# A backbone layer on one core: where the scans' loads lie, when the inverse's rounds are issued, and one lasting slot for wide weights

## The chip, the cores and the metric

One Trainium2 chip, one of its cores. The metric is the device time of one execution in microseconds. The kernel before ran three times: 1548.43, 1549.96 and 1550.71 us, median 1549.96 us.

## The reference, cut to what matters

One layer over 1024 latent tokens and 256 context tokens of width 1024. All products are in float32 precision (the kernel splits each float32 operand into a high and a low part and multiplies three times).

```python
px = modulate(rms_norm(x, norm1_w), sh1, sc1) @ w_in      # latent, 3600 columns
pc = modulate(rms_norm(ctx, norm1_w), csh1, csc1) @ w_in  # context
# group A: gated DeltaNet, 4 heads of 128
q, k, v = SiLU(conv5(...)); q, k = l2_normalize(q), l2_normalize(k); z, a, b from the same projection
m = where(strict_lower, (b*k) @ k.T * decay, 0)           # per chunk
u, w = solve(I + m, ...)                                  # triangular, per chunk and direction
S, o = scan over chunks, forward and backward, context first
dn_x = rms_norm(o_f + o_b) * silu(z)
# group B: 8 heads of 64, a query sees an 8 x 16 window of the 64-wide grid and all context keys
na_x = softmax([q k_win + rpb, q k_ctx]) @ [v_win, v_ctx]
x = x + g1 * (concat(dn_x, na_x) @ w_out)
x = x + g2 * swiglu(modulate(rms_norm(x, norm2_w), sh2, sc2), w_ffn_in, w_ffn_out)
```

## The kernel before, in words

**Stages.** The kernel projects all tokens in a list of jobs, then runs the two scans with the window attention filled in between, then multiplies with `w_out`, and then runs the feed-forward part.

**Jobs.** `jobs` is a list. A `Block` is one block of 128 output columns for all tokens (conv blocks `k`, `q`, `v`, and attention blocks `nk`, `nq`); a `Wide` is 256 columns with tokens on the partitions (`z`, half 1 then half 0, and the attention's values `nv`, halves 0 and 1). The order is: k0, k1, k2, k3, z1, nk0, nk1, nk2, nv0, nk3, q0 to q3, nq0 to nq3, v0, nv1, v1, v2, v3, z0. At job n the weights of job n+1 are fetched (`prefetch`: a load on SP's queue into `wraw`, which has one buffer, then a high part by ACT and a low part by POOL), the matmuls of job n run, job n-1 is normed (`norm`) and the Block two back is finished (`finish`).

**Norm and finish.** `norm` of an `nk` block makes three matmuls of sums (line 492), each into a PSUM bank called `m`, of which there are two, and ACT takes the logarithm of each (line 493). `finish` of a `v` block transposes it (line 527), scales it on DVE (line 531) and stores it to `v_d` (line 535). `kx`, `cr`, `cacc` and `zt` are the convolution's buffers, in a pool `cp`.

**Background.** Between the matmuls of a job one step of a background generator is issued (two or three per tile of a `Wide`). First comes `block_inverses`: decay tables, 32x32 blocks, then 30 rounds of substitution on DVE in the tile `N` (lines 885 and 887; two rounds a step), transposes of `N` by TensorE (line 897), and stores to `x_d`. Then comes `preps`: for each of 10 chunks it builds masked decays (`rg` on POOL, line 957; a matmul into a bank `pr`, lines 967 and 968) and assembles inverse blocks (lines 987 and 998), stored to `at_d` and `y_d` (line 1010). The chunks after the first two wait until the four `q` blocks are in the set `done`.

**Wide weights.** z1, nv0 and nv1 take their split weights `zw` from a pool `zp`, which is closed together with the background's other pools (`late`) when v3 begins. Then a pool `sp1` is opened, in which z0's `zw` is placed (and after it, in the same slot, the scans' sum `oacc`), then the attention's first loads are issued (`next(fill)`), then z0's weights are fetched.

**Values for the attention.** After nv1, 64 DMAs on SP copy `nv_d` to `vw_d` in windows (line 1108), all four pairs of heads each.

**Scans.** The pools of the scans are placed over the freed projection pools: `sl` (loads) first, then `sw` (working tiles, and the loads of `v`). The first chunk of each direction begins with a product of `v` and `y` (line 1217); the loads are line 1165.

**Order.** The framework plans the order of each engine's and each queue's instructions from the order in the program and from when it takes each to be ready; on the chip each engine and each queue then keeps that order and waits in place.

Of the kernel before, what the change touches and what calls it, by code (L numbers as in the profile page):

```python
# [88 lines left out]
def hybrid(ctx, tc, a, dbg):  # L89
# [47 lines left out]
    mr = const("mr", [128, 5, 128], F32R)  # L137
    mneg = const("mneg", [128, 2, 128], F32R)

# [235 lines left out]
    with ExitStack() as bs:  # L375
# [32 lines left out]
        class Block:  # L408
# [64 lines left out]
            def norm(self):  # L473
# [8 lines left out]
                if kind == "q":  # L482
# [6 lines left out]
                    return  # L489
                for s0, n in self.segs:  # L490
                    p = bank()
                    pe.matmul(p[:, :n], M[C_BD2], r[:, s0:s0 + n], start=True, stop=True)
                    act.activation(r[:, s0:s0 + n], p[:, :n], AF.Ln, bias=b_eps, scale=1.0 / ND)
# [26 lines left out]
            def finish(self):  # L520
                kind, acc, i = self.kind, self.acc, self.i
                if kind in "kv":
                    vt = cp.tile([128, NCH, 128], F32, name="vt", tag="kx", bufs=3)
                    for g, m in ((0, 4), (4, 4), (8, 2)):
                        p = bank()
                        for c in range(m):
                            pe.transpose(p[:, c * 128:(c + 1) * 128], acc[:, (g + c) * 128:(g + c + 1) * 128], ident)
                        if kind == "k":
                            act.copy(vt[:, g:g + m].rearrange("p c d -> p (c d)"), p[:, :m * 128])
                        else:  # L530
                            dve.tensor_tensor(vt[:, g:g + m], p[:, :m * 128].rearrange("p (c d) -> p c d", d=128),
                                              SV[:, g:g + m, i:i + 1].to_broadcast([128, m, 128]), OP.mult)
                        yield
                    dst = v_d if kind == "v" else k_d
                    sp.dma_start(dst[:, i * 128:(i + 1) * 128].rearrange("(c p) d -> p c d", p=128), vt)
                if kind == "q":
# [27 lines left out]
        class Wide:  # L564


            def __init__(self, kind, half, zp):
                self.kind, self.half, self.zp = kind, half, zp
                self.n = 272 if kind == "z" and half else 256
                self.lasting = kind == "z" and not half  # L570

            def room(self):
                w = self.zp().tile([128, 2, KT, 256 if self.lasting else 272], F32R, name="zw", tag="zw")
                self.hi, self.lo = w[:, 0], w[:, 1]

            def prefetch(self):
                h2, n = 2 * self.half, self.n // 2
                src = a["w_nv"] if self.kind == "nv" else a["w_z%d" % self.half]
                if self.kind == "z":
                    h2 = 0  # L580
                if not self.lasting:
                    self.room()
                for i in range(2):
                    raw = wp.tile([128, KT, 136], F32, name="wraw", tag="wraw", bufs=1)
                    r, s = raw[:, :, :n], slice(i * n, i * n + n)
                    sp.dma_start(r, src[h2 + i])
                    act.copy(self.hi[:, :, s], r)
                    pool.tensor_tensor(self.lo[:, :, s], r, self.hi[:, :, s].bitcast(F32), OP.subtract)
# [10 lines left out]
            def tiles(self):  # L599
# [18 lines left out]
                for t in range(2, NCH):  # L618
                    p = self.wide(t, 0, self.n)
                    if half == 0:  # L620
                        if t % 4 == 2:
                            zg = cp.tile([128, NCH, 128], F32, name="zg", tag="kx", bufs=3)
                            zg = zg.rearrange("p a b -> p (a b)")[:, :1024]
                        act.copy(zg[:, (t - 2) % 4 * 256:(t - 2) % 4 * 256 + 256], p[:, :256])
# [19 lines left out]
        with ExitStack() as xs:  # L644
# [65 lines left out]
            with tc.manual_schedule(engines={mybir.EngineType.PE, mybir.EngineType.DVE, mybir.EngineType.Activation}):  # L710
# [30 lines left out]
                for k in range(1, KT):  # L741
# [12 lines left out]
                    if k == 5:  # L754
                        act.copy(mr[:, 4], ident)
                        for d in range(2):
                            act.mul(mneg[:, d], masks[:, d], -1.0e30)
                        act.copy(mr[:, 0:4], masks)

        cp = pools(bs, "cp", "right")  # L760
        late = ExitStack()
        adp = pools(late, "adp", "left")
        zpool = [pools(late, "zp", "left")]
        first_half = ExitStack()
        cpa = pools(first_half, "cpa", "left")
        WK = cpa.tile([128, 2, NU, 32], F32, name="WK", tag="WK")
        KKc = WK[:, 1]

        def zp():
            return zpool[0]  # L770

# [53 lines left out]
        def block_inverses():  # L825
            with ExitStack() as gs:
# [55 lines left out]
                for c in range(30, 0, -1):  # L882
# [4 lines left out]
                    dve.tensor_tensor(N[:P, :, 0:c, c + 1:32], N[:P, :, 0:c, c + 1:32], t, OP.add)  # L887
                    if c % 2:
                        yield
                flat = N.rearrange("p b r c -> p b (r c)")  # L890
                dve.memset(flat[:P, :, 0:1024:33], 1.0)
                yield
                U = WK.rearrange("p d u i -> p (d u) i")
# [23 lines left out]
        def preps():  # L917

            first_half.close()
            with ExitStack() as gs:  # L920
# [28 lines left out]
                def prep(i, got):  # L949
# [9 lines left out]
                    for d, c, kk, xc, at in got:  # L959
                        for q in q32:  # L960
                            act.copy(fxs[d][q, :, q], xc[q, 1])
                    yield 1
                    es = []
                    for d, c, kk, xc, at in got:
# [64 lines left out]

        jobs = first + [Block("k", 2), Block("k", 3), Wide("z", 1, zp)]  # L1030
        inv = len(jobs)
        jobs += [Block("nk", i) for i in range(3)] + [Wide("nv", 0, zp), Block("nk", 3)]
        turn = len(jobs)
        jobs += [Block("q", i) for i in range(4)]
        later = len(jobs)
        queries = range(turn, later)
        jobs += [Block("nq", i) for i in range(4)] + [Block("v", 0), Wide("nv", 1, zp)]
        values = len(jobs) - 1
        jobs += [Block("v", i) for i in (1, 2, 3)] + [Wide("z", 0, zp)]

# [11 lines left out]
        for n in range(2, len(jobs) + 2):  # L1052
# [7 lines left out]
            if n == len(jobs) - 2:  # L1060
                bg.drain()
                bg2.drain()
                late.close()
                sp1 = pools(middle, "sp1", "left")
                zpool[0] = sp1
                jobs[n + 1].room()
                fill = attention(pools(attn, "nw", "left", 2))
                next(fill)
# [22 lines left out]
            elif j:  # L1091
                for k in range(KT):
                    j.mm([k])
                    if k >= 3:
                        next(fin, 0)
                    bg.step(1)
# [5 lines left out]
            done.add(n - 2)  # L1102
            if isinstance(j, Wide) and n == values:
                vlat = nv_d[CT:].rearrange("(r c) d -> r c d", c=64)
                for cb in range(4):
                    for ch in range(4):
                        for r in range(4):
                            sp.dma_start(vw_d[r * 32:r * 32 + 32, :, cb, ch],
                                         vlat[4 * ch + r, BLKS[cb]:BLKS[cb] + 32].rearrange("c (h d) -> c h d", d=128))
            if nrm:  # L1110
# [30 lines left out]

    with ExitStack() as gs:
        sl = pools(gs, "sl", "right", 3)
        shift(gs, "spad", "right", 16)
        sw = pools(gs, "sw", "right", 2)
        gs.callback(scan_psum.close)
# [14 lines left out]
        def load(d, c, near):  # L1161

            def tile_of(name, src):
                t = work(name, 3) if name == "v" else sl.tile([128, 4, 128], F32, name=name, tag=name)
                sp.dma_start(fl(t), src)
# [612 lines left out]
```

## Time and profile before

| | |
|---|---|
| median of three runs | 1549.96 us |
| the profiled execution | 1549.54 us |
| its span, first to last instruction | 1547.5 us |
| TensorE (PE) busy | 1479.8 us, 96% |
| VectorE (DVE) busy | 994.3 us, 64% |
| ScalarE (ACT) busy | 727.7 us, 47% |
| GpSimd (POOL) busy | 233.6 us, 15% |
| mean granted clock of TensorE | 0.982 |

A view by windows gives for each stretch of the span how long each engine was busy, the granted clock of TensorE (PEclk, 1.00 is full) and the share of the DMA engines in use. In a timeline, each row is: start, duration, engine, line, operation, tiles written <- tiles read, shapes, and in brackets how long the engine had been idle before and what ended that. SPq and ACTq are the queues from which SP and ACT issue DMAs.

### The profile page before, as it was taken

How to read it: one execution, taken by the hardware profiler on the slowest of the kernel's cores; microseconds unless marked ns; L12 is line 12 of the kernel's file. 1: busy time of each engine (PE TensorE's matmuls, PEld its weight loads, DVE VectorE, ACT ScalarE, POOL GpSimd, SP SyncE). 2: the span in 40 equal slices, each digit the busy share in tenths (PEclk: the TensorE clock that was granted, in tenths of full speed). 3: DMA queues.
4: the chain of work that ended last, by engine and by line, in shares of the span. 5: the costliest groups of instructions: out<-in, count | busy, mean ns of one | idle time of the engine just before them, and what ended most of it. 6: DMA issues, size and time to landing. Idle time of an engine off the chain costs nothing. (4 is left out here: it accounts for less than half of the span.)

```text
span 1547.5 us, 23963 instructions
## 1 busy us (share of the span) xinstructions
PE 1479.8 (96%) x8702; PEld 1235.2 (80%) x8702; DVE 994.3 (64%) x1712; ACT 727.7 (47%) x1404; POOL 233.6 (15%) x286
## 2 busy tenths in 40 slices
PE   6999999899989978999999999999999999999998
PEld 3788787678778867888887878888888888888887
DVE  5774497675554543777986469866665556599652
ACT  5442552635764235666773166333333334354440
POOL 1154500733554010111210000000000000000000
PEclk9999999999999979999999999999999999999999
DMA  9274221577556467899637502632323324698742
GB/s 389 64 217 133 67 72 63 163 212 241 182 169 212 130 174 237 283 288 261 220 102 255 208 34 82 211 102 103 103 102 103 109 100 159 231 381 279 244 144 82
DMA packets 204118, 267.35 MB, mean 173 GB/s; under 512 B 16736, under 2 KB 114528, under 8 KB 202976
## 3 DMA queue, kind: packets, MB, share of 16 engines
q1 hardware_dynamic: 198480, 261.07, 51.7%
q10 hardware_dynamic: 5520, 4.76, 0.9%
q8 instruction: 68, 1.11, 0.3%
q14 instruction: 50, 0.41, 0.1%
HBM read 201.02 MB, written 68.94 MB: 174 GB/s over the span
## 5 line engine op out<-in xcount | busy, mean ns | idle before, releaser
L405 PE MATMUL blk<-hh,whi 128*128 128x512 f32 (+1 forms) x410 | 123.4, 395 | 2.3 <-ACT kk L550 1.4
L1415 ACT CAST uhi<-wq 128x512 fp32r<-128x512 f32 x101 | 61.0, 622 | 133.5 <-issue 84.6
L1415 ACT CAST uhi<-ws 128x512 fp32r<-128x512 f32 x91 | 53.9, 621 | 147.3 <-PE ps L1354 92.9
L405 PE MATMUL blk<-hl,whi 128*128 128x512 f32 (+1 forms) x410 | 116.8, 377 | 0.3 <-DVE hl L707 0.3
L595 PE MATMUL blk<-zw,hh 128*128 128x256 f32 (+1 forms) x576 | 115.0, 293 | 1.3 <-ACT kk L550 1.1
L405 PE MATMUL blk<-hh,wlo 128*128 128x512 f32 (+1 forms) x410 | 114.7, 377 | 0.6 <-POOL wlo L200 0.6
L1416 DVE TENSOR_TENSOR ulo<-wq,uhi 128x512 fp32r<-128x512 f32 x101 | 67.4, 687 | 59.1 <-ACT uhi L1415 34.0
L1354 PE MATMUL ps<-hT,uhi 128*128 128x512 f32 x336 | 103.7, 390 | 0.0
L1354 PE MATMUL ps<-hT,ulo 128*128 128x512 f32 x336 | 103.5, 389 | 0.0
L1354 PE MATMUL ps<-lT,uhi 128*128 128x512 f32 x336 | 103.4, 389 | 0.0
L595 PEld LDWEIGHTS blk<-zw,hh 128*128 128x128 f32 x576 | 92.8, 192 | 5.2 <-ACT kk L550 1.4
L1354 PE MATMUL ps<-hB,uhi 128*128 128x512 f32 x288 | 89.2, 391 | 0.6 <-ACT hB L1529 0.6
L1354 PE MATMUL ps<-lB,uhi 128*128 128x512 f32 x288 | 88.7, 389 | 0.4 <-DVE lB L1530 0.4
L1354 PE MATMUL ps<-hB,ulo 128*128 128x512 f32 x288 | 88.7, 389 | 0.0
L405 PEld LDWEIGHTS blk<-hh,wlo 128*128 128x128 f32 x410 | 72.6, 192 | 15.3 <-POOL wlo L200 0.9
L405 PEld LDWEIGHTS blk<-hl,whi 128*128 128x128 f32 x410 | 72.4, 191 | 14.5 <-DVE hl L707 0.8
L405 PEld LDWEIGHTS blk<-hh,whi 128*128 128x128 f32 x410 | 69.4, 194 | 18.2 <-issue 4.5
L595 PE MATMUL blk<-zw,hl 128*128 128x256 f32 (+1 forms) x288 | 83.2, 289 | 0.0
L1354 PEld LDWEIGHTS ps<-lT,uhi 128*128 128x128 f32 x336 | 63.1, 188 | 13.1
L1354 PEld LDWEIGHTS ps<-hT,ulo 128*128 128x128 f32 x336 | 63.1, 188 | 13.1
L1354 PEld LDWEIGHTS ps<-hT,uhi 128*128 128x128 f32 x336 | 62.9, 188 | 13.0
L200 POOL TENSOR_TENSOR wlo<-wraw,whi 128x1024 fp32r<-128x1024 f32 x18 | 44.7, 2485 | 179.2 <-ACT whi L199 160.7
(359 smaller groups left out, 3540.5 us busy)
## 6 DMA issues: line engine op xcount, KB each, us to landing
wq<-w_fo SPq DMA_DIRECT2D x99, 256.0 KB, 4.2
wq<-w_gu SPq DMA_DIRECT2D x88, 256.0 KB, 2.9
wad<-wa SPq DMA_DIRECT2D x64, 256.0 KB, 4.4
bt<-rpb SPq DMA_DIRECT2D x64, 192.0 KB, 3.8
t_d<-g SPq DMA_DIRECT2D x22, 512.0 KB, 3.6
fr<-t_d SPq DMA_DIRECT2D x44, 256.0 KB, 5.0
f_d<-g SPq DMA_DIRECT2D x33, 256.0 KB, 2.1
fr<-f_d SPq DMA_DIRECT2D x33, 256.0 KB, 3.8
```

The source lines that it names most:

```text
L200: lo_engine.tensor_tensor(o, r, h.bitcast(F32), OP.subtract)
L405: pe.matmul(o, ww[:, k], xx[k][:, s], start=k == 0 and j == 0, stop=k == KT - 1 and j == 2)
L595: pe.matmul(p[:, :c1 - c0], x[k][:, s], ww[:, k, c0:c1], start=k == 0 and j == 0, stop=k == KT - 1 and j == 2)
L1354: pe.matmul(o, w[wi][:, k], x[xi][:, k], start=first and k == 0 and j == 0, stop=k == n - 1 and j == 2, skip_group_check=True)
L1415: act.copy(hi, self.raw[key])
L1416: dve.tensor_tensor(lo, self.raw[key], hi.bitcast(F32), OP.subtract)
```

## The change

It makes these edits:

- The third segment of an `nk` norm uses a bank `pr` instead of a third turn of the two `m` banks.
- `v` blocks are stored to `v_d` from ACT's queue; `k` blocks stay on SP's.
- All four `Wide` jobs take `zw` from one pool `sp1`, opened before the background's pools and lasting to the end of the scans, in one slot of 272 columns. The tile `mneg` moves from the constants to the pool of the modulation.
- z0's output tile `zg` moves from the buffers `kx` to the buffers `cr`.
- The inverse issues one round a step instead of two, and has four empty steps instead of one before the transposes of `N`.
- The first prep has one more empty step before its first matmul.
- A block counts as done when its `finish` is exhausted, instead of at the end of the job.
- The copies to `vw_d` are made in two halves: 64 DMAs after nv0 for two pairs of heads, 64 after nv1 for the other two.
- In the scans, `sw` is placed first and `sl` after it, so that `sl` lies over `cp`; `v` moves from `sw` to `sl`, three buffers as before.

```diff
-                for s0, n in self.segs:
-                    p = bank()
+                for j, (s0, n) in enumerate(self.segs):
+                    p = bank("pr" if j == 2 else "m")
                     pe.matmul(p[:, :n], M[C_BD2], r[:, s0:s0 + n], start=True, stop=True)
...
-                    sp.dma_start(dst[:, i * 128:(i + 1) * 128].rearrange("(c p) d -> p c d", p=128), vt)
+                    (act if kind == "v" else sp).dma_start(dst[:, i * 128:(i + 1) * 128].rearrange("(c p) d -> p c d", p=128), vt)
...
             def room(self):
-                w = self.zp().tile([128, 2, KT, 256 if self.lasting else 272], F32R, name="zw", tag="zw")
+                w = sp1.tile([128, 2, KT, 272], F32R, name="zw", tag="zw")
...
-                if not self.lasting:
-                    self.room()
+                self.room()
...
-                            zg = cp.tile([128, NCH, 128], F32, name="zg", tag="kx", bufs=3)
-                            zg = zg.rearrange("p a b -> p (a b)")[:, :1024]
+                            zg = cp.tile([128, T], F32, name="zg", tag="cr", bufs=2)
+                            zg = zg[:, :1024]
...
         late = ExitStack()
+        sp1 = pools(middle, "sp1", "left")
         adp = pools(late, "adp", "left")
-        zpool = [pools(late, "zp", "left")]
+        mneg = adp.tile([128, 2, 128], F32R, name="mneg", tag="mneg")
+        for d in range(2):
+            act.mul(mneg[:, d], mr[:, d].bitcast(F32), -1.0e30)
...
                     dve.tensor_tensor(N[:P, :, 0:c, c + 1:32], N[:P, :, 0:c, c + 1:32], t, OP.add)
-                    if c % 2:
-                        yield
+                    yield
                 flat = N.rearrange("p b r c -> p b (r c)")
                 dve.memset(flat[:P, :, 0:1024:33], 1.0)
-                yield
+                for _ in range(4):
+                    yield
...
                     yield 1
+                    if i == 0:
+                        yield 1
                     es = []
...
                 late.close()
-                sp1 = pools(middle, "sp1", "left")
-                zpool[0] = sp1
-                jobs[n + 1].room()
                 fill = attention(pools(attn, "nw", "left", 2))
...
-                    if k >= 3:
-                        next(fin, 0)
+                    if k >= 3 and next(fin, 0) == 0:
+                        done.add(n - 2)
...
-            if isinstance(j, Wide) and n == values:
+            if isinstance(j, Wide) and j.kind == "nv":
+                hv = slice(2 * j.half, 2 * j.half + 2)
                 vlat = nv_d[CT:].rearrange("(r c) d -> r c d", c=64)
                 for cb in range(4):
                     for ch in range(4):
                         for r in range(4):
-                            sp.dma_start(vw_d[r * 32:r * 32 + 32, :, cb, ch],
-                                         vlat[4 * ch + r, BLKS[cb]:BLKS[cb] + 32].rearrange("c (h d) -> c h d", d=128))
+                            rows = vlat[4 * ch + r, BLKS[cb]:BLKS[cb] + 32].rearrange("c (h d) -> c h d", d=128)
+                            sp.dma_start(vw_d[r * 32:r * 32 + 32, hv, cb, ch], rows[:, hv])
...
     with ExitStack() as gs:
+        sw = pools(gs, "sw", "right", 2)
+        shift(gs, "spad", "right", 16)
         sl = pools(gs, "sl", "right", 3)
-        shift(gs, "spad", "right", 16)
-        sw = pools(gs, "sw", "right", 2)
...
-                t = work(name, 3) if name == "v" else sl.tile([128, 4, 128], F32, name=name, tag=name)
+                t = sl.tile([128, 4, 128], F32, name=name, tag=name)
```

More of the change, by code (lines that the diff above doesn't have):

```diff
@@ L137, in hybrid @@
     mr = const("mr", [128, 5, 128], F32R)
-    mneg = const("mneg", [128, 2, 128], F32R)
     v_d = dram.tile([T, 512], F32, name="v_d", tag="v_d")
@@ L564, in hybrid, with __init__ @@
         class Wide:
-            def __init__(self, kind, half, zp):
-                self.kind, self.half, self.zp = kind, half, zp
+            def __init__(self, kind, half):
+                self.kind, self.half = kind, half
                 self.n = 272 if kind == "z" and half else 256
-                self.lasting = kind == "z" and not half
             def room(self):
-                w = self.zp().tile([128, 2, KT, 256 if self.lasting else 272], F32R, name="zw", tag="zw")
+                w = sp1.tile([128, 2, KT, 272], F32R, name="zw", tag="zw")
                 self.hi, self.lo = w[:, 0], w[:, 1]
@@ L755, in hybrid @@
                         act.copy(mr[:, 4], ident)
-                        for d in range(2):
-                            act.mul(mneg[:, d], masks[:, d], -1.0e30)
                         act.copy(mr[:, 0:4], masks)
@@ L767, in hybrid @@
         KKc = WK[:, 1]
-        def zp():
-            return zpool[0]
         def decay_tables(gp):
@@ L1028, in preps @@
                 flush(tick[0] + 2)
-        jobs = first + [Block("k", 2), Block("k", 3), Wide("z", 1, zp)]
+        jobs = first + [Block("k", 2), Block("k", 3), Wide("z", 1)]
         inv = len(jobs)
-        jobs += [Block("nk", i) for i in range(3)] + [Wide("nv", 0, zp), Block("nk", 3)]
+        jobs += [Block("nk", i) for i in range(3)] + [Wide("nv", 0), Block("nk", 3)]
         turn = len(jobs)
@@ L1036, in hybrid @@
         queries = range(turn, later)
-        jobs += [Block("nq", i) for i in range(4)] + [Block("v", 0), Wide("nv", 1, zp)]
+        jobs += [Block("nq", i) for i in range(4)] + [Block("v", 0), Wide("nv", 1)]
         values = len(jobs) - 1
-        jobs += [Block("v", i) for i in (1, 2, 3)] + [Wide("z", 0, zp)]
+        jobs += [Block("v", i) for i in (1, 2, 3)] + [Wide("z", 0)]
         def blk(n):
```

## The prediction, made before the changed kernel ran

> **What bounds the kernel now.** I read the page first, then the span cut at its stages, then TensorE's waits, then the timeline where those waits lie.
>
> ```profile
> span 1547.5 us, 23963 instructions
> PE 1479.8 (96%) x8702; PEld 1235.2 (80%) x8702; DVE 994.3 (64%) x1712; ACT 727.7 (47%) x1404; POOL 233.6 (15%) x286
> ```
>
> The profiled execution took 1549.54 us, 2.0 more than its span; the median of the three runs is 0.4 above it. TensorE is the bound. An edit that adds no product and takes none away can only act on the time in which TensorE stands or runs at a lower clock. The stages show where that is (cut at nk0's start, nk3's end, nq0, v3's end, z0's end, the scans' settling, `w_out`):
>
> ```profile
> core 0: us, PE busy (x) PEld busy (x) DVE busy (x) ACT busy (x) POOL busy (x), PEclk, DMA share, GB/s
> 141.00:250.00 109.00, 102.19 (x604) 87.54 (x605) 83.20 (x100) 45.11 (x70) 32.35 (x26) 0.98 0.21 61
> 250.00:345.00 95.00, 84.53 (x468) 67.28 (x468) 62.00 (x64) 46.25 (x79) 42.06 (x43) 0.89 0.52 163
> 345.00:497.00 152.00, 143.28 (x1045) 119.31 (x1044) 84.49 (x106) 90.24 (x169) 72.69 (x88) 1.00 0.66 205
> 549.00:596.00 47.00, 36.36 (x269) 33.06 (x270) 20.29 (x31) 17.02 (x28) 5.27 (x4) 0.82 0.60 169
> 596.00:613.00 17.00, 11.85 (x85) 9.38 (x83) 8.38 (x18) 13.72 (x28) 1.25 (x4) 0.80 1.03 330
> 613.00:813.00 200.00, 196.38 (x1870) 172.91 (x1868) 153.98 (x472) 141.41 (x396) 32.78 (x66) 1.00 0.75 232
> 813.00:1547.50 734.50, 728.70 (x3228) 601.72 (x3224) 476.02 (x763) 290.71 (x499) 2.59 (x2) 1.00 0.47 160
> ```
>
> From 813 on the change touches nothing and TensorE stands 5.8 of 734.5 us. In the five stages from 141 to 613 shown here it stands 6.8 + 10.5 + 8.7 + 10.6 + 5.2 = 41.8 us, and the lower clock costs a further (1 - PEclk) of each stage: 2.2 + 10.5 + 0 + 8.5 + 3.4 = 24.6 us. These 66 us are all that can be won, and the waits with names are these (sum, times, longest):
>
> ```profile
> PE m L492 <- ACT cr L493: 5.3, 4, 1.4
> PE sc L303 <- DVE mx L305: 5.7, 4, 4.1
> PE sc L303 <- DMA kh<-nk_d: 4.5, 1, 4.5
> PE sc L314 <- DVE bt L309: 3.4, 3, 2.3
> PE pr L967 <- POOL rg L957: 2.9, 3, 1.2
> PE m L897 <- DVE N L891: 2.9, 1, 2.9
> PE ps L1217 <- DMA y<-y_d: 2.3, 2, 1.6
> ```
>
> **The change part by part.**
>
> **Norm's third bank.** Four `nk` norms wait once each, 5.3 us in all, because the third product needs a `m` bank that ACT still reads. A third bank removes just that; `preps`, the other user of `pr`, has not begun in the first three norms. Bounds 0 (the wait moves to the next block's banks) and 5.3; I take 5, since ACT is busy 45 of 109 us in that stage and empties the next banks in time.
>
> **Rounds and empty steps.** The rounds are a chain on DVE, and TensorE meets its end:
>
> ```profile
> 195.29 0.37 DVE L885 TENSOR_TENSOR tt<-N 80x120 f32<-80x120 f32 x1 [3.67 <-ACT N L877]
> 257.70 0.45 PE L897 MATMUL m<-cst,N 80*128 80x80 f32 x2 [2.89 <-DVE N L891]
> 258.22 0.28 DVE L887 TENSOR_TENSOR N<-N,tt 80x120 f32<-80x120 f32 x1
> 258.50:266.00 7.50, 7.50 (x40) 6.70 (x39) 1.09 (x2) 3.41 (x8) 0.00 (x0) 0.54 0.05 18
> 289.50:293.00 3.50, 3.50 (x10) 2.71 (x9) 3.11 (x4) 3.35 (x8) 3.29 (x5) 0.51 1.03 344
> ```
>
> One round a step and three more empty steps put the transposes 18 steps later in the program (a step is some 2.1 us: nk0 to nk3 and nv0 have 4 x 8 + 20 = 52 in the 109 us of their stage), near to where they run anyway, with matmuls of q0 in front of them. The wait of 2.9 us costs more than itself: the clock is 0.54 for the 7.5 us behind it, 3.45 us lost. So 6.3 us are there to win. But the chain still ends near 258, and TensorE comes some 4 us earlier by the norms. Bounds: a loss of 4 and a gain of 6.3; I take 4. The Trainium skill ("TensorE: Matmul & The Clock Gate", section "Why this matters for your kernels") advises to leave no idle gap over about 3 us; read as a limit, this gap would cost 2.9 alone. The trace disagrees, and its 6.3 stands. That `preps` begin 18 steps later costs nothing: their first two chunks need some 18 steps (nine a chunk) from step 62, and the others wait for the `q` blocks until about step 98 of the background, which the earlier `done` moves forward by some three steps.
>
> **First prep's empty step.** The three waits for `rg` (2.9 us) and the clock of 0.51 over 3.5 us behind them (1.7 lost) make 4.6. One step of 2 us covers one wait of 1.2 and perhaps the clock. Bounds 0 and 4.6; I take 2.
>
> **z0's weights.** Here most is at stake. The three attention waits of up to 4.5, 4.1 and 2.3 us stand at 548 to 563, between v3 and z0, where TensorE has attention products only because z0's weights are late:
>
> ```profile
> 495.88 36.09 SPq L1108 DMA_DIRECT2D vw_d<-nv_d  x53
> 517.64 2.38 POOL L200 TENSOR_TENSOR wlo<-wraw,whi 128x1024 fp32r<-128x1024 f32 x1 [17.36 <-PE pr L998]
> 535.68 0.61 SPq L586 DMA_DIRECT2D wraw<-w_z  x1
> 548.13 1.35 ACT L453 COPY cr<-blk 128x256 f32<-128x256 f32 x3 [5.77 <-PE blk L405]
> 549.35 1.07 ACT L587 CAST zw<-wraw 128x1024 fp32r<-128x1024 f32 x1
> 555.34 0.60 SPq L586 DMA_DIRECT2D wraw<-w_z  x1
> 563.15 2.37 POOL L588 TENSOR_TENSOR zw<-wraw,zw 128x1024 fp32r<-128x1024 f32 x1 [10.31 <-ACT zw L587]
> 565.57 0.80 PE L595 MATMUL blk<-zw,hh 128*128 128x256 f32 x2
> t_d<-g SPq DMA_DIRECT2D x22, 512.0 KB, 3.6
> ```
>
> `wraw` is free at 520.0, when POOL has split v3's weights. Its load goes out at 535.68, behind the 53 copies to `vw_d` and the last preps' stores; its cast stands on ACT behind v3's evacuation; and the second half's load stands behind the attention's loads. With half of each copy's bytes gone and the slot lasting, the fetch depends on SP alone. One half takes a landing of 3.6 us (the row of another 512 KB load), a cast of 1.07 and a split of 2.4, so two take 14.2. If the copies, as many as before, still end at 532, the weights stand at 546.2, before v3 ends at 548.5. The gain is then 4.5 + 4.1 + 2.3 = 10.9 of idle and (1 - 0.82) of 47 us, 8.5, of clock: 19.4. If the second half's load still lies behind the attention's fourteen loads (some 8 us at 0.6), 5.7 us of wait and one slow stretch remain. Bounds 0 and 19.4; I take 16, nearer to the upper end, because the chain fits with 2 us to spare even with slow copies.
>
> **Scans' loads.** Between 596 and 613 TensorE stands 5.2 us and loses 3.4 by the clock, 8.6 in all.
>
> ```profile
> 596.43 0.39 SPq L535 DMA_DIRECT2D v_d<-vt  x1
> 602.13 0.32 SPq L1165 DMA_DIRECT2D v<-v_d  x1
> 607.16 1.13 PE L1217 MATMUL ps<-v,y 128*128 128x128 f32 x8 [0.66 <-DMA y<-y_d]
> DMA to landing us min/median/max: 4.1/5.3/6.9
> ```
>
> Over `cp` the loads of `kt`, `y` and `kT` need no longer wait for z0's last matmul. But `v` has its own chain: v3's store at 596.43 takes 4.1 to 6.9 us to land (last row, the `v_d` and `k_d` stores), just when the load of `v` goes out. That stays. So the first product comes some 3 us earlier. Bounds 0 and 8.6; I take 4.
>
> **What is added.** 64 more DMAs on SP after nv0: at 36.09 / 53 = 0.68 us each, 44 us of its queue. The last of the values leaves at 236.12 (below) and lands some 2 us later, so the copies reach to about 282.
>
> ```profile
> 236.12 0.33 ACTq L606 DMA_DIRECT2D nv_d<-zt  x1
> 253.36 0.59 SPq L195 DMA_DIRECT2D wraw<-w_conv  x1
> 269.49 1.04 ACT L199 CAST whi<-wraw 128x1024 fp32r<-128x1024 f32 x1 [4.61 <-PE blk L405]
> 291.23 1.05 PE L405 MATMUL blk<-hh,whi 128*128 128x512 f32 x2
> L1108 SPq DMA_DIRECT2D vw_d<-nv_d x64: 469/596/1811, 461.0 to 531.4; - x64
> ```
>
> What is queued behind them is q2's weights: issued at 253.36, cast at 269.49, used at 291.23. At 282 they would still be split by 289.1 (7.1 as above). I cost it at nothing; the cover is two microseconds. The four `v_d` issues on ACT take some 0.4 us each and wait there for DVE's line 531; behind them stand z0's evacuations, which have slack while ACT is busy 17 of 47 us. `mneg`, `zg` and the slot's width cost nothing. The 8.7 us of small waits in the steady preps (345 to 497) are dealt anew; I book a loss of 3, bounds a gain of 4 and a loss of 10.
>
> The sum: 5 + 4 + 2 + 16 + 4 - 3 = 28 us, so 1549.5 - 28 = 1521.5.
>
> **The rivals.**
>
> A: z0's weights stay late. If a half copy holds SP as long as a whole one and the order after nv1 stays as it is, the fetch still goes out at 535 with its cast behind v3's evacuation. Then 12 us remain: 1537.5. For it: the issues number the same and last 469 to 1811 ns each. Against it: the chain above. By the Trainium skill ("DMA: Bandwidth & Descriptors", sections "Rules for kernel authors" and "Issuing engines are not separate DMA queues") small transfers should be coalesced, and issuing from another engine saves only sequencer time: by that rule the halves bring nothing, and this rival holds. The trace bears it out in so far as SP's issue time is the resource here.
>
> B: slower. SP becomes the bound after nv0. If the copies take over 0.7 us each, q2's weights come late, 6.4 us for each 0.1. At 1.2 us they come 31 us late and the whole gain is gone; at 1.4 us the burst ends at 328, the weights stand at 335 instead of 291, and with the clock it is 1549.5 - 28 + 44 + 4 = 1569. For it: the longest took 1.8 us, and `x_d`'s stores and the preps' loads fall into the same stretch. Against it: DMA share is 0.21 there, and eleven of the 64 went out during nv1, between its tiles.
>
> C: the waits only move. The norms' next wait, the transposes' and the prep's come back at the same size one product later, and z0's are made up by first scores waiting on DVE, which works off v3's convolution then: about 1549.
>
> D: all terms at their upper end, 5.3 + 6.3 + 4.6 + 19.4 + 8.6 = 44: 1505.
>
> **How the numbers follow.** The forecast has 0.62, A 0.18, B 0.09, C 0.06, D 0.05. A measurement of this kernel can tell about 0.2%, 3 us. Faster: 0.62 + 0.18 + 0.05 and a third of C, 0.87; same: a third of C, 0.02; slower: B and the rest, 0.11. The range leaves out B, C and D, 0.20, and reaches from just above D over A's 1537.5 to what A becomes when the other unknown costs stand at their lower bounds for the rounds (8 less): 1506 to 1546.
>
> **What would show it.** Right: line 492 gone from TensorE's waits; the wait of line 897 under 1 us; z0's matmuls following v3's within 2 us at full clock; the first product of line 1217 some 9 us after z0's last instead of 12. Wrong: z0's cast still behind v3's evacuation (A); SP's row of copies reaching past 290 with a wait for `wlo` or `whi` at q2 (B); the same idle under new names (C).

## The result, and the profile after

The changed kernel takes 1541.84 us in the median of 20 runs (1538.35 to 1545.18), the kernel before, on the same chip, 1549.66 us (1540.4 to 1554.14, 20 runs). The ratio is 0.9955, 95% interval 0.9944 to 0.9966. That is 7 to 8 us faster where 28 were forecast. The profiled execution took 1544.97 us with a span of 1542.8, so the pair of profiles shows 4.7 of these us.

First the page of the changed kernel, then its span cut at the prediction's stages (columns: stretch, length, busy time of each engine with instructions, TensorE's granted clock, DMA share, GB/s):

```profile
span 1542.8 us, 24027 instructions
PE 1475.4 (96%) x8702; PEld 1231.8 (80%) x8702; DVE 994.6 (64%) x1712; ACT 728.4 (47%) x1405; POOL 234.4 (15%) x286
```

```profile
141.00:250.00 109.00, 104.26 (x620) 89.12 (x621) 84.53 (x100) 47.45 (x73) 35.29 (x27) 1.00 0.27 76
250.00:345.00 95.00, 83.39 (x482) 66.71 (x482) 72.90 (x72) 45.30 (x76) 41.12 (x42) 0.93 0.62 187
345.00:497.00 152.00, 143.69 (x1046) 119.88 (x1046) 73.64 (x99) 94.81 (x179) 74.17 (x95) 0.97 0.64 195
497.00:549.00 52.00, 45.60 (x280) 37.77 (x279) 22.99 (x30) 12.78 (x19) 7.71 (x7) 0.93 0.60 164
549.00:596.00 47.00, 41.63 (x343) 37.96 (x342) 21.54 (x44) 21.16 (x37) 2.06 (x6) 0.99 0.46 134
596.00:613.00 17.00, 13.95 (x116) 11.21 (x115) 9.59 (x24) 10.25 (x29) 0.94 (x3) 0.93 0.84 278
```

The norm's stage (141 to 250) and z0's (549 to 596) look as hoped: 2.1 us more of busy TensorE in the one, 5.3 more in the other, and the clock of 0.82 is gone. But in the stage in front of z0 (497 to 549) TensorE now stands 6.4 us, at 0.93. Before, it was full at clock 1.00:

```profile
497.00:549.00 52.00, 51.50 (x336) 41.84 (x334) 23.68 (x35) 15.08 (x30) 5.75 (x13) 1.00 0.42 125
```

The steady preps (345 to 497) run at 0.97 instead of 1.00. TensorE's waits in the changed kernel name the new places (sum, times, longest):

```profile
PE pr L995 <- ACT kk L987: 7.7, 7, 2.1
PE blk L404 <- ACT cr L452: 6.3, 1, 6.3
PE m L892 <- DVE N L885: 5.6, 1, 5.6
PE pr L984 <- DVE kk L971: 2.9, 1, 2.9
PE pr L964 <- POOL rg L952: 2.0, 3, 1.0
PE ps L1212 <- DMA y<-y_d: 1.7, 1, 1.7
```

Lines have moved: 404 is the blocks' product (405 before), 592 z0's (595), 892 the inverse's transposes (897), 964 and 984 the preps' (967, 987), 995 the next (998), 1104 the copies (1108), 1212 the scans' first product (1217). The waits of line 492 are gone; all others but those for `rg` and `y` are new or longer.

A ledger sums it up. It goes by marks in the timelines (first and last products of the blocks); length of each stretch in us, and what it won against before. The last column is the best kernel of the experiments.

| from, to | before | after | won | forecast | joined copies, `v_d` on SP, old `done`, v last |
|---|---|---|---|---|---|
| start, nk0's first product | 141.6 | 141.2 | 0.4 | 0 | 140.8 (0.8) |
| nk0's first, nk3's last | 108.1 | 104.6 | 3.5 | 5 | 104.7 (3.4) |
| nk3's last, nq0's first | 94.6 | 90.9 | 3.7 | 6 | 89.2 (5.4) |
| nq0's first, v1's first | 152.3 | 158.0 | -5.7 | -3 | 155.6 (-3.3) |
| v1's first, scans' first product | 110.5 | 108.2 | 2.3 | 20 | 96.9 (13.6) |
| scans' first product, end | 940.3 | 939.8 | 0.5 | 0 | 940.4 (-0.1) |

A stretch also changes when a background product crosses its edge, so rows that stand together are safer than one. Even so, 17.7 of the 23.3 us that are missing are missing between v1 and the scans. That row has four parts (before, after): v1's first product to v3's last, 51.9 and 59.1; from there to z0's first, 14.9 and 1.0; z0's products, 31.8 and 30.7; z0's last to the scans' first, 12.0 and 17.5. So the wait for z0's weights went as forecast, and most of what it won was lost again on both sides of it.

### The profile page after: what moved, and what is told of

It reads as the page before. It is cut to its first block, busy times and chain, and to the rows that moved or that the text cites. A ratio compares the mean times of both kernels' runs of the same rounds, so it can differ in the third digit from the quotient of the medians.

```text
span 1542.8 us, 24027 instructions
## 1 busy us (share of the span) xinstructions
PE 1475.4 (96%) x8702; PEld 1231.8 (80%) x8702; DVE 994.6 (64%) x1712; ACT 728.4 (47%) x1405; POOL 234.4 (15%) x286
## 5 line engine op out<-in xcount | busy, mean ns | idle before, releaser
L1410 ACT CAST uhi<-ws 128x512 fp32r<-128x512 f32 x91 | 54.0, 621 | 146.6 <-PE ps L1349 96.9
L1349 PE MATMUL ps<-hB,uhi 128*128 128x512 f32 x288 | 89.2, 391 | 0.6 <-ACT hB L1524 0.6
L404 PEld LDWEIGHTS blk<-hl,whi 128*128 128x128 f32 x410 | 72.9, 193 | 14.9 <-DVE hl L704 0.8
```

What stands on the lines that cost most here:

```text
L404: pe.matmul(o, ww[:, k], xx[k][:, s], start=k == 0 and j == 0, stop=k == KT - 1 and j == 2)
L1349: pe.matmul(o, w[wi][:, k], x[xi][:, k], start=first and k == 0 and j == 0, stop=k == n - 1 and j == 2, skip_group_check=True)
L1410: act.copy(hi, self.raw[key])
```

## The experiments

**Four theories** stood before the first experiments. 1: a copy holds SP equally long whatever its bytes, so z0's weights still come late, and their cast, now planned on ACT ahead of v2's evacuation, stops v3 instead of z0. 2: the norm's gain only brings TensorE earlier to a DVE chain whose end does not move. 3: v3's store on ACT holds up the scans' loads. 4: the earlier `done` sets off the waits of 2 us in the steady preps. Unless said otherwise each kernel is the changed kernel with one edit. Gains between kernels are differences of ratios to before, times 1549.7 us; each has an uncertainty of 3 to 5 us, so a gain below that can't be told from none by the time alone.

These lines of the changed kernel carry theory 1 (timeline of SP, ACT, POOL and TensorE; in brackets the idle time before and what ended it):

```profile
492.38 30.91 SPq L1104 DMA_DIRECT2D vw_d<-nv_d  x46
526.98 0.61 SPq L583 DMA_DIRECT2D wraw<-w_z  x1
533.00 1.04 ACT L584 CAST zw<-wraw 128x1024 fp32r<-128x1024 f32 x1 [14.92 <-DMA wraw<-w_z]
536.53 1.33 ACT L452 COPY cr<-blk 128x256 f32<-128x256 f32 x3
536.93 0.79 PE L404 MATMUL blk<-hh,whi 128*128 128x512 f32 x1 [6.34 <-ACT cr L452]
554.85 0.39 PE L592 MATMUL blk<-zw,hh 128*128 128x256 f32 x1 [1.03 <-ACT cr L452]
```

46 half copies take 30.91 us of SP, 0.67 each; whole ones took 36.09 / 53 = 0.68. The fetch goes out at 526.98, ACT stands 14.92 us until it has landed, and v1's Silu and v2's evacuation stand behind the cast. So v3 finds no free bank for 6.34 us. z0 itself follows v3 by 1.03. (In the seven kernels below that leave this place alone the same wait takes 4.2 to 5.5 us.)

**u_whole**: the copies whole again, after nv1.

```diff
-            if isinstance(j, Wide) and j.kind == "nv":
-                hv = slice(2 * j.half, 2 * j.half + 2)
+            if isinstance(j, Wide) and n == values:
+                hv = slice(0, 4)
```

> The change with one part undone: the copies to vw_d are 64 whole ones after nv1 again. Theory 1 (each copy holds SP's queue as long whether whole or half, so halving the bytes only moved the cast of z0's weights ahead of v2's evacuation in ACT's planned order, where it now waits 14.9 us for SP): the cast stands behind v2's evacuation, v3's wait of 6.3 us for its banks goes, z0's weights come 10 us late instead, as before; 1545 to 1550 us. Rival (the halves shorten the queue and bring the weights early by themselves): the same late weights but with the loads later by half the burst, some 15 us: 1555 or more. If the halves are indifferent: 1542.

1549.15 us, ratio 1.0001 (0.998 to 1.0022). Its cast and waits:

```profile
527.30 1.35 ACT L452 COPY cr<-blk 128x256 f32<-128x256 f32 x3 [1.84 <-PE blk L404]
540.44 1.05 ACT L584 CAST zw<-wraw 128x1024 fp32r<-128x1024 f32 x1 [3.55 <-DVE vt L530]
```

```profile
PE sc L302 <- DVE mx L304: 8.1, 2, 7.1
PE sc L313 <- DVE bt L308: 3.7, 3, 2.5
```

With whole copies the cast stands behind v2's evacuation, v3 does not wait, and the attention waits of before are back. So the halves are worth 7.1 us, although they shorten no issue and 64 DMAs stand behind nv1 either way. The fetch leaves 35.8 us after v1's first product with whole copies and 32.2 with halves (527.79 and 526.98 on the clock), but the cast comes 48.4 after it with whole copies and 38.2 with halves. Most of this is the cast's place on ACT: with whole copies it stands behind v2's evacuation, a Silu and a store to `v_d`.

**c_coal**: the halves, with the four `r` of a head in one DMA, 32 of 64 KB instead of 64 of 32 KB per half.

```diff
-                        for r in range(4):
-                            rows = vlat[4 * ch + r, ...]...
-                            sp.dma_start(vw_d[r * 32:r * 32 + 32, hv, cb, ch], rows[:, hv])
+                        for h in range(2 * j.half, 2 * j.half + 2):
+                            sp.dma_start(vw_d[:, h, cb, ch].rearrange("(r c) d -> c r d", c=32), ...)
```

> The change with the copies to vw_d joined: each DMA takes four image rows of one head pair, so 32 DMAs of 64 KB stand after nv0 and 32 after nv1, where 64 of 32 KB each stood. Theory 1: SP is free some 15 us sooner after nv1 (32 issues at 0.6 to 0.7 us), ACT no longer waits 14.9 us for z0's first weights, v3's wait of 6.3 us goes and z0 follows at full clock; 1531 to 1536 us. Rival (the landing under load, not the issue, holds the weights, so the bytes count): 1540 to 1543, the wait stays.

1536.2 us, ratio 0.9916 (0.9887 to 0.9944), 6.0 us better than the changed kernel.

```profile
489.66 13.88 SPq L1103 DMA_DIRECT2D vw_d<-nv_d  x20
521.37 0.61 SPq L583 DMA_DIRECT2D wraw<-w_z  x1
529.16 1.07 ACT L584 CAST zw<-wraw 128x1024 fp32r<-128x1024 f32 x1
```

A joined copy of twice the bytes takes 13.88 / 20 = 0.69 us of SP. With half as many the fetch goes out sooner (28.7 us after v1's first product), the cast waits for nothing, and v3's wait of 6.3 us is gone. SP is held by the number of DMAs and not by their bytes, as theory 1 says. But two things changed here: the cast also stands behind v2's evacuation again. x_coal_vsp below has the joined copies with the changed kernel's order on ACT (cast, table load, Silu, evacuation): its fetch leaves 24.5 us after v1's first product, and v3 waits 0.95 us. So with the cast ahead of the evacuation it is the late load that makes v3 wait.

**u_vsp**: the values' blocks stored from SP again.

```diff
-                    (act if kind == "v" else sp).dma_start(dst[...], vt)
+                    sp.dma_start(dst[...], vt)
```

> The change with one part undone: v blocks are stored to v_d from SP's queue. Theory 3 (v3's store stood on ACT behind a table load, Silu, copies and an Exp, some 5 us after its last scaling, and the scans' first product hangs on it): the store goes out within 1 us of DVE's last scaling, the first product comes 5 us sooner after z0's end, 12 us instead of 17; 1537 to 1540 us. Rival (the attention fills that time anyway): 1541 to 1543. If stores on SP hold the attention's loads back again: 1544 or more.

1536.43 us, ratio 0.9922 (0.9897 to 0.9948), 5.1 us better. The changed kernel shows why:

```profile
585.93 1.28 ACT L623 ACT_TABLE_LOAD   x1
588.19 0.68 ACT L316 COPY pt<-sc 128x640 f32<-128x640 f32 x1
590.43 1.28 ACT L306 ACT_TABLE_LOAD   x1
591.73 0.39 ACTq L534 DMA_DIRECT2D v_d<-vt  x1
596.98 0.33 SPq L1160 DMA_DIRECT2D v<-v_d  x1
597.41 0.37 SPq L1160 DMA_DIRECT2D kt<-k_d  x1
602.98 1.16 PE L1212 MATMUL ps<-v,y 128*128 128x128 f32 x8 [1.68 <-DMA y<-y_d]
```

On ACT v3's store stands behind z0's Silu, attention copies and two table loads. It goes out at 591.73, 6.2 us after z0's last product at 585.5, and the scans' loads stand behind it on SP. The first product comes 17.5 us after z0's last. With the store on SP it comes 13.8 us after it (577.94 to 591.78):

```profile
579.16 0.39 SPq L534 DMA_DIRECT2D v_d<-vt  x1
591.78 2.05 PE L1212 MATMUL ps<-v,y 128*128 128x128 f32 x8 [3.50 <-DMA y<-y_d]
```

Theory 3 holds, but it is only half of the gain: of the 7.0 us by which the stretch from v1 to the scans is shorter in this profile, 3.6 lie behind z0 and 3.3 at v3, whose wait is 3.0. ACT's timelines show why. Here the table load and v1's Silu (together 2.5 us) stand ahead of the cast, in time that ACT would spend waiting for the load anyway; in the changed kernel they stand between the cast and v2's evacuation. The load also lands 1.5 us faster, though it leaves 0.8 us later after v1's first product.

**u_done**: the background's `done` at the job's end again.

```diff
-                    if k >= 3 and next(fin, 0) == 0:
-                        done.add(n - 2)
+                    if k >= 3:
+                        next(fin, 0)
```

> The change with one part undone: a block counts as done only at the end of its job. Theory 4 (the new waits of up to 2 us for kk between 370 and 442, and the three slow stretches behind them, 5 us, come from the chunks being taken earlier into the nq jobs): they go, the clock in that stage is 1.00 again; 1535 to 1539 us. Rival (they come from elsewhere, as the copies or the later inverses shift all preps): the waits at line 995 stay, 1541 to 1543.

1537.94 us, ratio 0.9924 (0.9904 to 0.9945), 4.8 us better. But not as theory 4 had it: the 2-us waits of line 995 go and others come (2.77 at line 984, 1.22 at 404), the clock from 345 to 497 stays 0.97, and that stretch is only 2.4 us shorter. Most of the rest is v3's bank wait, 2.6 instead of 6.3: against v1's first product the fetch leaves 1.9 us sooner, with fewer copies and one store to `y_d` less ahead of it, and it lands 1.2 us faster. The size was right and the place half wrong.

**u_norm**: the third bank taken back (`p = bank()`).

> The change with one part undone: the third product of a nk norm takes a bank m again. Theory 2 (in the stage up to the transposes the chain of rounds on DVE is the bound, so what the norms save TensorE stands at the transposes): the four waits of 1.3 us at line 491 come back, the wait for N falls from 5.6 to about 2.5 us and its slow stretch gets shorter; 1541 to 1545 us. Rival (the norms' 5.3 us are won for good): 1547.

1543.56 us, ratio 0.9965 (0.9944 to 0.9985): the edit is worth 1.5 us, less than the uncertainty. The waits trade places:

```profile
PE m L491 <- ACT cr L492: 5.2, 4, 1.4
PE m L892 <- DVE N L885: 2.2, 1, 2.2
```

5.2 us of waits come back, and the wait for the rounds falls from 5.6 to 2.2: DVE's chain ends near 258 with or without the edit (258.0 and 258.5). Theory 2 holds.

**e_empty8**: eight empty steps instead of four, to put more products in front of the transposes.

```diff
-                for _ in range(4):
+                for _ in range(8):
                     yield
```

> The change with eight empty steps before the transposes of N instead of four. Theory 2 (TensorE reaches the transposes 5.6 us before the chain on DVE ends, and only products put in front of them help): the wait for N falls below 1 us and the slow stretch of 10 us behind it goes, some 10 us in all; part of it returns at the first prep's waits for rg, since the preps come four steps later; 1533 to 1537 us. Rival (the inverse's end sets the preps, and TensorE stands there for the same time instead): 1541 to 1543.

1543.95 us, ratio 0.9959 (0.9942 to 0.9977), no gain:

```profile
PE m L491 <- ACT WK L894: 5.6, 1, 5.6
```

The wait for `N` is gone, and the norm waits as long for `m` banks that the later transposes hold. The rival was right.

**u_rounds**: two rounds a step and one empty step again.

```diff
-                    yield
+                    if c % 2:
+                        yield
...
-                for _ in range(4):
-                    yield
+                yield
```

> The change with one part undone: two rounds a step, one empty step before the transposes of N. Theory 2 (the chain of rounds is bound by DVE, and the transposes stand where N is planned to be ready, whatever the steps): the transposes stay at the same place in TensorE's order and wait 5 to 6 us for N again; 1540 to 1543 us. Rival (the step count places them, so the wait grows without it): a wait of 8 us or more, 1546.

1554.58 us, ratio 1.0038 (1.0015 to 1.006). Undoing the edit costs 12.9 us in the medians, 6.1 in the profiled spans, and neither theory nor rival had the size. The wait for `N` (6.4) stands where it stood; the loss is in the first preps' stage, the third row of this cut:

```profile
250.00:345.00 95.00, 80.94 (x446) 64.32 (x446) 57.33 (x58) 43.26 (x77) 45.44 (x58) 0.89 0.54 171
```

Against the changed kernel TensorE does 2.5 us less there, at 0.89 instead of 0.93, and nq0 begins at 344.6 instead of 336.8. What of the edit does this was still open, so three kernels took it apart.

**r_two_e19**: two rounds a step and 19 empty steps, which keeps the delay of the transposes and preps and undoes the dealing of the rounds.

> The changed kernel with two rounds a step again, and 19 empty steps instead of 4, so that the transposes and all preps come in the same step as in the changed kernel (15 + 19 = 30 + 4). Theory (the delay of what follows is the whole edit; DVE's chain runs as fast as it can either way and ends near 258): ratio to before 0.993 to 0.998, the changed kernel's 0.9955, and nq0 starting near 337. Rival (the dealing of the rounds is what pays): as with the edit undone, ratio 1.001 to 1.006, nq0 near 344.

1542.61 us, ratio 0.9962 (0.9949 to 0.9974), nq0 at 337.7: the same as the changed kernel. So how the rounds are dealt out does not matter; the number of steps does.

**r_one_e1**: one round a step and one empty step, 15 of the 18 steps.

> The changed kernel with one round a step and one empty step instead of four: 15 of the 18 steps of delay are kept. Theory (the delay): most of the gain stays, ratio 0.995 to 0.999, nq0 near 338. Rival (only the last steps matter, because they put matmuls in front of the transposes): ratio 1.001 or more.

1551.17 us, ratio 1.0023 (1.0006 to 1.0041), nq0 at 346.0. My theory, that most of the gain would stay, fell: three steps fewer lose all of it. The rival's number came but not its reason: the wait for `N` is 5.8 us, as in the changed kernel (5.6). The largest wait that the changed kernel does not have can be followed (DVE's timeline, then TensorE's):

```profile
315.02 0.29 DVE L996 COPY y<-pr 32x128 f32<-32x128 f32 x1
321.99 0.75 DVE L233 SCALAR_TENSOR_TENSOR acc<-wad,sc,acc 128x512 f32<-128x512 f32 x1 [6.68 <-DMA wad<-wa]
322.77 0.42 DVE L996 COPY y<-pr 32x256 f32<-32x256 f32 x1
323.25 1.57 PE L994 MATMUL pr<-y,kk 128*32 128x96 f32 x16 [4.77 <-DVE y L996]
```

DVE stands 6.68 us at an instruction of another task (line 233) whose load has not landed; the prep's copy is the next on DVE, and TensorE waits 4.77 us for it. Three steps later the prep meets other neighbours. This wait, at least, is a matter of which instructions fall together, not of a step's price; what makes up the rest of the 10 us is not shown.

**b_rounds**: the kernel before with this edit alone.

> The kernel before with this edit alone: one round a step, four empty steps. Theory (the delay pays in the first preps' stage, whatever the norms do): 6 to 13 us faster, ratio 0.991 to 0.996. Rival (it pays only where the other edits have moved work next to it; the forecast's own 4 us at the wait): ratio 0.997 or more.

1545.44 us, ratio 0.9982 (0.9966 to 0.9998): 2.8 us faster. The rival was right: alone, the edit is worth about the 4 us of the forecast. Beside the other edits, taking it back costs some 10 us more than that.

**u_first** and **u_slsw**: the first prep's empty step taken out; and the scans' pools in the old order, `v` in its old buffers.

> The changed kernel without the first prep's empty step. Theory (the step moved one wait of 1 us and brought one of 2.9 at the next product): within 1.5 us of the changed kernel, 1540.5 to 1543, waits for rg back at 2.9. Rival (the prediction's 2 us): 1544.

> The changed kernel with the two pools of the scans in the old order (loads not over the convolution's buffers, v in a buffer of work). Theory (the first load of v goes out behind v3's late store on ACT, 17 us after z0's last matmul, and the others behind it on SP, so the place of the buffers decides nothing): 1541 to 1543, first product of the scans still about 17 us after z0. Rival (the place does matter, as the prediction's 3 to 4 us): 1545 to 1546.

u_first: 1541.74 us, ratio 0.9961 (0.9943 to 0.9978). The waits for `rg` are 3.0 instead of 2.0, that at the next product 0.9 instead of 2.9; the step is worth nothing that can be measured. u_slsw: 1539.46 us, ratio 0.9948 (0.9928 to 0.9967): as long as v3's store is on ACT, where the scans' buffers lie decides nothing, and the first product comes 16.2 us after z0. With the store on SP the old place was not tried.

**x_coal_vsp, x_coal_vsp_done, x_done_vlast**: the good edits put together; the last also asks for `v` behind `kt`, `y` and `kT`.

> The change with the joined copies (32 after each nv) and with the v blocks stored from SP's queue. Theories 1 and 3 name two different places (v3's banks and the scans' first product), so the gains of 5.6 and 5.4 us add: 1530 to 1532 us. Rival (both act through the cast's place on ACT, so one is most of the other): 1535 to 1536.

> The joined copies, v's store on SP, and the earlier done put back. Theory (the new costs lie on three waits: v3's bank wait behind SP's copies, the scans' start behind ACT's queue, and the small waits of the preps that an earlier done sets off): joined copies and v_d on SP gave 1533.8, and since both and the done share v3's bank wait, which is already down to 1 us there, the done can only add what it costs elsewhere: 1531 to 1533. Rival (the three costs are independent, 5.6 + 5.4 + 4): 1541.8 - 15 = 1527.

> As the run before, with the scans' first loads in another order: kt, y and kT of each first step ahead of v. Theory (over the convolution's buffers these three need not wait for z0, only SP's order behind v's load, which follows v3's store, holds them): they go out some 2 us sooner, but v's own load, the last of the chain, does not, so the first product comes no sooner and the time is the same within 2 us. Rival (the row of loads, 0.43 us each, is itself the chain): the first product some 3 us sooner and the time 2 to 3 us lower.

They take 1533.84 (ratio 0.9898, 0.9877 to 0.9919), 1532.55 (0.9895, 0.9876 to 0.9914) and 1530.32 us (0.9886, 0.9865 to 0.9908). Joined copies and `v_d` on SP together bring 8.8 of their 6.0 + 5.1, which is within the uncertainty of the sum. The old `done` adds 0.5 instead of 4.8 once v3's wait is small (0.95), so it shared that wait with the others. The order of the loads is within the uncertainty; the first product comes 12.1 us after z0 in the last kernel and 12.2 in the one before it, now released by `v` itself. In the last kernel's stretch from v1 to the scans (cut at 497, 549 and 613) TensorE stands 2.3 and 7.5 us, where the changed kernel's stands 6.4 and 8.4, and the clock is full:

```profile
497.00:549.00 52.00, 49.66 (x324) 41.32 (x323) 31.60 (x40) 14.56 (x23) 8.88 (x7) 1.00 0.63 182
549.00:613.00 64.00, 56.53 (x518) 50.82 (x518) 33.21 (x83) 38.11 (x83) 5.14 (x13) 1.00 0.65 209
```

This kernel is 1.1% faster than before and beats the changed one by 0.7%.

## Why the prediction was wrong in its size

The sign was right, and the time fell into the range, at its slow end. That it did is in part luck: the slow end was made of rival A and 8 us, and A did not come as it was pictured. By its steps, the largest errors first:

- **The scans' loads, 4, and the four `v_d` issues on ACT, costed at nothing.** From z0's last product to the scans' first it took 12.0 us before and 17.5 after: 5.5 lost where 4 were forecast. The step that failed is the cover for the issues: I named what stands behind them (z0's evacuations) and not what stands ahead of them, nor who waits for the store: the scans' load of `v`, and on SP all loads behind it. Put back on SP, the store brings 5.1 us, some of it at v3's wait. The term of 4 failed by itself, too. The forecast says of `v`'s own chain "That stays" and takes 3 us off all the same. In the four kernels with the store on SP the first product comes 11.3 to 13.8 us after z0's last, 12.0 before, and where `v` is loaded last it is `v` that it waits for.
- **z0's weights, 16.** The gain came where it was forecast: from v3's last product to z0's first it is 1.0 us instead of 14.9, at clock 0.99, and the attention waits went. "The chain fits with 2 us to spare" was right, too: the weights stand at 549.5, and v3 ends at 553.8. The step that failed goes with "the fetch depends on SP alone": the cast's place on ACT is left out, and what the cast holds up there while it waits stands at nothing, although the forecast had named ACT's order as what made the cast late before. Now the cast stands ahead of v2's evacuation, and ACT's wait of 14.92 us became v3's 6.34, with the clock at 0.78 for the 8 us behind it (next fence). From v1's first product to v3's last it takes 7.2 us longer, and from v1's first to z0's last only 7.8 of the 16 are won. With joined copies that stretch is 15.9 us shorter than before. The bound of 19.4 was too high in any case: it added the idle time to the clock's loss over the whole stage, 8.5, of which only 4.9 us fall on time in which TensorE was busy (stage of before in windows of 1 us).

```profile
530.00:537.00 7.00, 0.66 (x5) 0.30 (x3) 0.08 (x1) 3.98 (x5) 3.01 (x4) 0.76 1.08 260
537.00:545.00 8.00, 8.00 (x33) 6.72 (x34) 7.65 (x10) 1.03 (x3) 0.00 (x0) 0.78 1.03 290
```

- **Rival A** gave 1537.5 on the ground that a half copy holds SP as long as a whole one. That is what the copies do, 0.67 against 0.68 us, and joining them brought 6.0. The Trainium skill's advice in "DMA: Bandwidth & Descriptors", section "Rules for kernel authors", to coalesce small transfers, is borne out by these 6.0 us. A's picture failed in two things: the fetch left at 526.98 and not at 535, and the cast was not behind v3's evacuation but ahead of v2's, so the wait moved to v3.
- **The norm's bank, 5.** The waits went as forecast, but its worth is 1.5, if anything: 3.4 us of the gain were spent at the DVE chain's end, as its own sentence "the chain still ends near 258" said. I put that into the bounds of the next term instead of into the value of this one.
- **Rounds and empty steps, 4.** Alone it won 2.8, as sized, but hardly at the wait for `N`, which fell from 2.9 to 2.2 there (and grew to 5.6 in the changed kernel). The profile of b_rounds has more work and a higher clock (0.95 instead of 0.89) in the first preps' stage. What the edit is worth beside the others (12.9) no row of before showed.
- **First prep's step, 2.** Nothing: one us left `rg`, two came at the next product.
- **What is added, -3.** The steady preps lost 5.7, and the earlier `done`, which the forecast only used as an argument for the preps' start, cost 4.8 by the time, much of it elsewhere (in the profiles 2.4 of 6.9 us lie in the steady preps).
- **Rival B** did not come: the copies after nv0 took 0.65 us each, about the forecast's 0.68, but 23 of the 64 had gone out before, so q2's fetch left at 259.05 instead of 282:

```profile
232.45 26.50 SPq L1104 DMA_DIRECT2D vw_d<-nv_d  x41
259.05 0.59 SPq L194 DMA_DIRECT2D wraw<-w_conv  x1
```

- **Rival C** was half right: three waits moved one engine or one product on, at about their size.

The parts measured one by one (7.1 + 12.9 + 1.5 + 0.9 - 1.1 - 5.1 - 4.8) make 11.4 against 7.0 for the whole: within their uncertainties, and they interact. No run takes out the lasting slot, or the new places of `zg` and `mneg`, alone, so what these are worth is not known; the slot has a part in z0's early weights that was not measured. Open, too, is which of the neighbours in the first preps' stage cost u_rounds its 13 us.

## What to carry to other kernels

When a late transfer is made earlier, follow not only its data but every in-order queue in which its consumers and its store stand: a cast that is planned earlier than its load can land stops all that is queued behind it, and a store on a busy engine leaves when that engine gets there. Count DMAs, not bytes, where a queue issues them one by one. And before a wait is booked as a gain, ask what TensorE meets next and whether that moves too.

## What the runs showed of the hardware

- A copy's time on SP did not depend on its bytes: 0.67 us for 32 KB, 0.68 for 64 KB whole, 0.69 for 64 KB joined.
- A wait of 2 us can be enough for the clock to fall. After the wait of 2.01 us at 396.81 the granted clock of the changed kernel was 0.57 over the next 4 us, then 1.00:

```profile
393.00:397.00 4.00, 1.99 (x12) 1.32 (x10) 0.68 (x1) 3.97 (x5) 1.06 (x4) 1.00 0.77 236
397.00:401.00 4.00, 3.76 (x24) 3.03 (x23) 2.19 (x4) 3.86 (x12) 0.00 (x0) 0.57 0.15 35
401.00:404.00 3.00, 3.00 (x27) 2.21 (x26) 0.42 (x1) 1.45 (x3) 1.76 (x1) 1.00 0.58 133
```

  This wait cost nearly twice itself (2.0 us and 1.7 by the clock), and so did the one of 2.07 us at 444.02 (0.61 over the next 4 us). But it is no rule. The kernel before has two longer waits in a stage whose clock was 1.00, and it stayed 1.00 behind them:

```profile
447.49 1.16 PE L987 MATMUL pr<-fx,kk 128*128 128x128 f32 x8 [2.54 <-ACT y L1001]
451.64 0.60 PE L987 MATMUL pr<-fx,kk 128*128 128x128 f32 x3 [2.29 <-ACT kk L990]
```

  What tells the two cases apart is not shown by these runs. The Trainium skill advises in "TensorE: Matmul & The Clock Gate", section "Why this matters for your kernels", to leave no idle gap over about 3 us; all four gaps here are shorter, and two of them were followed by a slow stretch.
